# A hybrid encoder layer: branch a's first output block with its token halves interleaved, branch b's operand queued behind the attention, a wider-spaced inverse, another PSUM bank for the last head

## The chip, the cores and the metric

The kernel runs on one core of one Trainium2 chip. The metric is the device time of one execution in microseconds; less is better. TensorE (PE) multiplies matrices, VectorE (DVE), ScalarE (ACT) and GpSimd (POOL) do the elementwise work, and SyncE (SP) issues the DMAs. PEld is the loading of weights into PE, which lies beside the matmuls.

## The reference

One layer over 1024 tokens of width 1024, in float32. One input projection feeds two branches: eight heads of a gated delta rule in chunks of 64 (branch a) and sixteen heads of attention over a band of nine chunks (branch b). Each branch is projected to 1024 columns and merged by gates; then come an output projection, a layer norm, and a feed-forward layer with a short convolution.

```python
h = x * (1.0 + scale_t) + shift_t
proj = h @ w_in
qkv_a, z_a, beta_raw, a_raw, q_b, k_b, v_b, gates = split(proj)
o_a = gated_deltanet(qkv_a, z_a, beta_raw, a_raw, ...)   # per chunk: a triangular solve, then a scan over chunks
o_b = chunk_band_attention(q_b, k_b, v_b, rel_bias)      # softmax over own chunk + previous 8
merged = gate_a * (o_a @ w_branch_a) + gate_b * (o_b @ w_branch_b)
x = layernorm(ALPHA * x + gate_t * (merged @ w_o))
h = x * (1.0 + scale_f) + shift_f
u = causal_dwconv(h @ w_up) + b_conv_ffn                 # width 3
x = layernorm(ALPHA * x + gate_f * ((silu(u_gate) * u_val) @ w_down))
```

## The kernel before

Every large matrix product is made of three: each float32 operand is split into a high part (a cast by ACT into the fast float32 format, `wh`, `hh`, `oah`, `obh`) and a low part (the rest, a subtraction by DVE or POOL, `wl`, `hl`, `oal`, `obl`), and high x high, high x low and low x high are summed in PSUM. `load_split` does this for one block: a DMA of 512 KB into one of three `raw` buffers (`RB`), the cast, the subtraction. `wblock` does it for a block of weights.

The program runs in stages, which overlap:

1. The modulation and the first projections.
2. The eight heads of branch a. While head h goes through its stages, `feed(h + 1)` projects the next head. PE's order is written out by hand: the projections are a stream of units (one matmul of 512 columns is one unit), and at given counts of units a stage is put in as a "wave". A head's waves are `stage_blocks` (copies of 32x32 blocks into `dd`, a transposition into `dt_`), four steps of `stage_inverse` (tiles `pxt`, `py`, `pzz`, `pT`) that build the inverse of a triangular matrix out of its blocks, 22 steps of `stage_chain` (the scan: `pks`, `pvn`, `pu`, `po`), and `stage_out` (the normalised output, transposed by way of `pt`, stored in `oa_d`). `INV0` and `INV00` say where the inverse begins (`INV00` for head 0), `INVS` how far apart its steps are, and the chain is spread evenly from there to the end of the head. The 31 small steps of `stage_solve` on DVE make the blocks' own inverses.
3. The attention of branch b: 64 groups g (head g // 4, two tiles of 128 tokens in each), with scores (`ps`), softmax (DVE's minimum, ACT's exponential), transposes of the weights (`pp`, split into `ph` by ACT and `pl` by DVE) and output (`po`). `fill_to` puts units of other work between these steps, from a list of items: what is left of branch b's own projections, and then the eight blocks of branch a's output projection (`branch_a(j)`, tile `pbr`, 48 units each: 24 for each half of the tokens). A block may start only behind a given group (49 for the first two, 60 for the others). `load(i + 1)` asks for the next item's weights as an item begins. The operand of branch a is read back from `oa_d` in eight parts by `operand(k)`, at the unit counts of `OAT`, counted from the middle of the last projection (`late(15, True)`); 24 is the beginning of `branch_a(0)`. `OL` lists the parts whose low half POOL makes instead of DVE.
4. The rest of `branch_a`, then the eight blocks of branch b's output projection, whose operand `obh`, `obl` is read back from `ob_d` in eight parts after blocks 5, 6 and 7 of `branch_a`.
5. Merge, output projection, layer norm, feed-forward layer, second layer norm.

The order of PE is kept as written from head 0's waves to the end of the attention (`lane.pinned`). On the other engines a scheduler, which simulates the program as it is built, chooses the order. `tc.high_priority` puts a wave's work ahead of others' there. `tc.issue_after(ins)` ties what is issued inside it behind `ins`, on the engine of `ins` alone. A PSUM bank is taken from a ring: `"a"` and `"qkv"` have banks 0 and 1, `"c"` (the chain and `pt`) and `"pt"` (the transposes `pp`) have banks 3 and 4; `turn` holds how often each ring was used.

Lines of the profile that the text speaks of: L190 and L179 subtract the low part (L187 and L176 are their casts; the first pair is for operands and weights loaded in cuts), L184 loads `raw`; L531 issues PE's work in the ordered part, L289 that of branch b's projection; L583 is the last step of the short convolution of q, k and v, L584 its activation; L736 multiplies q by the decay; L770 and L772 copy the blocks, L775 transposes them; L792, L793 and L809 copy results of the inverse; L839 and L845 are steps of the chain; L873 scales its output; L1117 multiplies branch a's block by its gate (tile `ma`), which frees the bank; L1212 and L1216 are the softmax, L1242 and L1243 the split of its transposed weights. The profile names a tile by the buffer that it lies in: G, FT, GT, SA, SB, ST, A, B are shared buffers, and `hh`, `hl` hold branch a's operand from stage 3 on.

Of the kernel before, what the change touches and what calls it, by code (L numbers as in the profile page):

```python
# [12 lines left out]
ALU = mybir.AluOpType  # L13
# [7 lines left out]
NK = 8  # L21
# [14 lines left out]
PTR = 0  # L36
G0 = 3
GA = (3, 2, 2, 2, 2, 2, 1)
INV0, INV00, INVS, OUT0, OUTS, TAIL0 = 38,188,14,14,8,10
WA, WB0 = 9, 10  # L40
EP = (4,12)
OAT = (2, 5, 8, 14, 20, 29, 33, 37)
OL = (1,3,5)
PO = ((1, 5, 2, 3, 7, 6, 4), (1, 5, 2, 3, 7, 6, 4))
ED = ((4,0),(5,0),(5,1),(6,0))
MS = 6
# [93 lines left out]
def hybrid_layer(  # L140
# [547 lines left out]
    def feed(h, n_gates, mods):  # L688

        c = cs[h]  # L690
        decay(h, c)
        k, q = Conv(h, 1), Conv(h, 0)
        c["kT"], c["qT"] = k.y, q.y
        yield from k.half(0)
        yield from k.half(1)
        c["kd"], c["ss"] = big("kd"), sm("ss", 2 * NT)
        yield from q.half(0)
        keys(h, c, 0)
        yield 2
        yield from q.half(1)  # L700
        keys(h, c, 1)
        yield 2
        rates(h, c)
        v = Conv(h, 2)
        c["vT"] = v.y
        mod = mod_rows(mods[0]) if mods else iter(())
        with tc.issue_after(cs[h - 2]["scaled"]) if mods else nullcontext():
            next(mod, None)
        yield from v.half(0)
        c["am"] = big("am")  # L710
        for g in range(2):
            gram(h, c, g)
            yield 4
        blocks_out(h, c)
        if h == 0:
            for key in ("kT", "qT"):
                dump(key, flat(c[key]))
        yield from v.half(1)
        if h == 0:
            dump("vT", flat(c["vT"]))  # L720
        c["at"] = big("at")
        for g in range(2):
            scores(h, c, g)
            yield 4
        c["sz"], szw = big("sz"), wblock(kview(w_in2, 3 * D + h * P, P), NK)
        for n in range(2):
            ps = dhalf(nm("pz"))
            yield from project(ps, szw, n)
            ACT.activation(flat(c["sz"])[:, 512 * n:512 * n + 512], ps, AF.Silu)
            if n == 0:  # L730
                for g in range(2):
                    queries(h, c, g)
                    yield 2
                eq = c["eq"] = sm("eq")
                DVE.tensor_scalar(eq, c["ss"][:, NT:], P * RMS_EPS, P * RMS_EPS * L2_EPS, ALU.mult, ALU.add)
                POOL.tensor_tensor(flat(c["qT"]), flat(c["qT"]), flat(c["gb"]), ALU.mult)  # L736
        c["vs"] = big("vs")
        for g in range(2):
            values(h, c, g)
            yield 2  # L740
        run(mod)
        for i in range(n_gates + 1):
            if i == (h == 1):
                with tc.high_priority(offset=PF):
                    stage_solve(h, c)
            if i < n_gates:
                yield from gate_block(next(gates))
# [13 lines left out]
    def stage_blocks(h, c):  # L761

        fr = c["fr"]
        for b in (1, 3, 0, 2):
            for q in range(4):
                dst = dd[B[b], :, 32 * b + 8 * q:32 * b + 8 * q + 8]
                s_ = fr[B[q], :, 8 * b:8 * b + 8].rearrange("p c t -> p t c")
                with nullcontext() if h else tc.issue_after(cs[1]["ready"]), tc.issue_after(cs[1]["keys"][1]):
                    if q % 2:
                        ACT.copy(dst, s_)  # L770
                    else:
                        DVE.tensor_copy(dst, s_)  # L772
        with tc.issue_after(cs[h - 1]["end"][0] if h else cs[1]["ready"]):
            for b in (1, 3, 0, 2):
                DVE.transpose(dt_[B[b], :, B[b]], dd[B[b], :, B[b]])  # L775
        yield
# [178 lines left out]
    for h in range(HA - 1):  # L955
# [6 lines left out]
        inv, chain = stage_inverse(h, cs[h]), stage_chain(h, cs[h])  # L962
        i0 = INV0 if h else INV00
        waves = [(stage_blocks(h, cs[h]), 0)] + waves if h else [(stage_blocks(h, cs[h]), i0 - 22)]
        waves += [(inv, i0 + INVS * i) for i in range(4)]
        c0 = i0 + 4 * INVS
        gaps = [WB0 if i % 3 == 0 else WA for i in range(22)]
        pos = [sum(gaps[:i]) for i in range(23)]
        waves += [(chain, c0 + (total - TAIL0 - c0) * p / pos[-1]) for p in pos]
# [11 lines left out]
    oah, oal = hh, hl  # L981
    oahk = [oah[:, k, :] for k in range(NK)]
    oalk = [oal[:, k, :] for k in range(NK)]
    vts, ma, keys_low, wb0 = {}, {}, [], []

    class Head:

# [112 lines left out]
    def branch_a(j):  # L1100

        def body(w):
            ma[j] = place(MA[j], [P, S], F32, "ma")
            if j == 0:
                turn["ps_a"] = turn["ps_qkv"]
            if j == 7:
                wb0.append(wblock(kview(wbr[1], 0, P), NK))
            for n in range(2):
                N = slice(512 * n, 512 * n + 512)
                ps = pbank(nm("pbr"), "a")  # L1110
                for u, _ in enumerate(project(ps, w, n)):
                    yield 1
                    if j == 0 and n == 0 and u + 24 in OAT:
                        operand(OAT.index(u + 24))
                gt_ = ma[j][:, N]
                SP.dma_start(gt_, gates_d[j][:, N])
                DVE.scalar_tensor_tensor(gt_, gt_, 1.0, ps, ALU.add, ALU.mult)  # L1117
            for k in {5: (0, 1, 2), 6: (3, 4, 5), 7: (6, 7)}.get(j, ()):
                load_split(obh[k], obl[k], ob_d[k], ACT, DVE)

        return lambda: wblock(kview(wbr[0], j * P, P), NK, cuts=2), body

# [2 lines left out]
    def fills(items):  # L1125

        ws = {}

        def load(i):
            while i < len(items) and i not in ws:  # L1130
                ws[i] = items[i][0]()
                if items[i][2]:
                    return
                i += 1
            while i in ws and not items[i][2]:
                i += 1

        load(0)
        for i, (_, body, units, after) in enumerate(items):
            if units:  # L1140
                load(i + 1)
            while group_no[0] < after:
                yield None
            yield from body(ws.pop(i))
# [124 lines left out]
    def vals(g):  # L1269
# [1 line left out]

    items = [first_pair("q"), first_pair("k"), vals(0), late(1), late(9), late(2), late(10), late(3), vals(1), late(11),
             late(5), vals(2), late(13), late(6), late(14), vals(3), late(7), late(15, True)]
    items += [(*branch_a(j), True, a) for j, a in enumerate((49, 49, 60, 60, 60, 60, 60, 60))]
    fill, done = fills(items), 0

    def fill_to(x):
# [9 lines left out]
    group("MX", "ST", 52)  # L1287
    waves = [(stage_blocks(h, cs[h]), 0)] + [(older, OUT0 + OUTS * i) for i in range(3)]
    inv, chain, last = stage_inverse(h, cs[h]), stage_chain(h, cs[h]), stage_out(h, cs[h])
    waves += [(inv, INV0 + INVS * i) for i in range(4)]  # L1290
    c0 = INV0 + 4 * INVS
    waves += [(chain, c0 + (total - TAIL0 - c0) * p / pos[-1]) for p in pos]
    ready = {}

# [35 lines left out]
    for g in range(8 * NK):  # L1330
# [16 lines left out]
            if h:  # L1347
                seq.insert(0, head(h + 1).load)
        if g == 0:
            seq = [head(1).bias, T[0], lambda: fill_to(done + 4), lambda: wave(last, PC), lambda: fill_to(done + 4),  # L1350
                   lambda: wave(last, PC), lambda: wave(last, PC), lambda: fill_to(done + 4)]
        for key in [k for k in due if g >= min(8 * k[0] + 8 + 2 * k[1], 8 * NK - 1)]:
            finish_part(key)
# [523 lines left out]
```

## Time and profile before

| what | value |
|---|---|
| median of 3 runs | 2171.91 us (2170.02 to 2172.66) |
| the profiled execution | 2167.07 us, span 2165.4 us |
| PE busy | 2108.1 us, 97% of the span |
| DVE, ACT, POOL busy | 1429.3 (66%), 987.7 (46%), 431.9 (20%) us |
| mean granted clock of PE | 0.994 |
| DMA | 263.03 MB, mean 121 GB/s |

The span is the time from the first to the last instruction of the profiled execution. A row of the order of time reads: start, duration, engine, line, operation, result and operands, and in brackets how long the engine had been idle before it and what ended that. A row of the waits reads: who waited, for whom, us in total, how many times, the longest. PE is the engine with next to no idle time, so a wait counts where PE has it; and where its granted clock is below 1, its busy time is longer than it need be.

### The profile page before, as it was taken

Reading aid. Unit: us, or ns where it says so; the run is one execution under the profiler, and the core shown is the slowest. Engines: PE = TensorE matmul, PEld = TensorE weight load, DVE = VectorE, ACT = ScalarE, POOL = GpSimd, SP = SyncE. Lnnn points to the kernel's source line nnn. Section 1 sums busy time; section 2 is a strip of 40 time slices with the busy share of each in tenths; the row PEclk is TensorE's granted clock in tenths of the full one; section 3 lists DMA queues with packets and bytes.
Section 4 is the critical chain, followed back from the end, with each engine's and each line's share of the span. In section 5 each row is a group of like instructions: output and inputs, shape, how many; then the busy total and the mean of one; then the engine's idle time right before and its main releaser. Section 6 shows DMA issues by size and latency. Waiting matters only on the chain. (4 is left out here: it accounts for less than half of the span.)

```text
span 2165.4 us, 31785 instructions
## 1 busy us (share of the span) xinstructions
PE 2108.1 (97%) x11577; PEld 1767.0 (82%) x11577; DVE 1429.3 (66%) x3006; ACT 987.7 (46%) x2159; POOL 431.9 (20%) x385
## 2 busy tenths in 40 slices
PE   7998999999999999999999899999999999999998
PEld 6787788888888888989897778888788888888886
DVE  6478576776777844666556432457997788875754
ACT  5544453454444434566555432235554444452431
POOL 0233233323232321111112124300120000000000
PEclk9999999999999999999999999999999999999999
DMA  9232324323233245554647442422232222275440
GB/s 296 81 89 80 123 76 120 115 74 119 80 104 122 80 125 160 139 136 111 174 120 229 122 142 93 141 88 85 82 98 78 88 88 87 87 282 186 165 156 39
DMA packets 243166, 263.03 MB, mean 121 GB/s; under 512 B 23034, under 2 KB 189491, under 8 KB 243011
## 3 DMA queue, kind: packets, MB, share of 16 engines
q1 hardware_dynamic: 242931, 260.99, 39.0%
q8 instruction: 91, 1.49, 0.3%
q14 instruction: 64, 0.52, 0.1%
q10 hardware_dynamic: 80, 0.03, 0.0%
HBM read 207.89 MB, written 58.83 MB: 123 GB/s over the span
## 5 line engine op out<-in xcount | busy, mean ns | idle before, releaser
L190 POOL TENSOR_TENSOR wl<-raw,wh 128x512 fp32r<-128x512 f32 x170 | 223.8, 1339 | 526.7 <-ACT wh L187 433.3
L1595 PE MATMUL pup<-hh,wop 128*128 128x512 f32 x704 | 224.2, 390 | 0.4 <-ACT G L1632 0.4
L1595 PE MATMUL pup<-t,wop 128*128 128x512 f32 x792 | 189.4, 392 | 1.3 <-DVE cc L1636 0.8
L1595 PEld LDWEIGHTS pup<-t,wop 128*128 128x128 f32 x792 | 148.6, 188 | 34.7 <-DVE cc L1636 1.2
L1749 PE MATMUL pdn<-dop,dop 128*128 128x512 f32 x696 | 161.6, 391 | 0.0
L1595 PEld LDWEIGHTS pup<-hh,wop 128*128 128x128 f32 x704 | 132.2, 188 | 29.0 <-ACT G L1632 0.8
L1749 PEld LDWEIGHTS pdn<-dop,dop 128*128 128x128 f32 x696 | 130.7, 188 | 28.3
L531 PE MATMUL pqkv<-hh,wh 128*128 128x512 f32 x352 | 142.6, 406 | 0.0
L531 PE MATMUL pqkv<-hl,wh 128*128 128x512 f32 x352 | 139.8, 397 | 0.0
L531 PE MATMUL pqkv<-hh,wl 128*128 128x512 f32 x352 | 139.7, 397 | 0.0
L1595 PE MATMUL pup<-hl,wop 128*128 128x512 f32 x352 | 137.2, 390 | 0.0
L187 ACT CAST wh<-raw 128x1024 fp32r<-128x1024 f32 x88 | 92.1, 1047 | 77.9 <-PE pbr L531 18.3
L1637 POOL TENSOR_TENSOR cc<-cc,G 128x512 f32<-128x512 f32 x22 | 44.1, 2004 | 375.6 <-DVE G L1619 352.4
L1216 ACT ACTIVATE G<-G,ST 128x640 f32<-128x640 f32 (+4 forms) x128 | 89.3, 698 | 60.8 <-DVE ST L1212 60.1
L176 ACT CAST wop<-wr 128x512 fp32r<-128x512 f32 x104 | 61.9, 620 | 99.2 <-DVE wr L1577 67.1
L531 PE MATMUL pqk<-hh,wh 128*128 128x512 f32 x256 | 105.9, 414 | 0.0
L531 PE MATMUL pqk<-hl,wh 128*128 128x512 f32 x256 | 104.1, 407 | 0.0
L531 PE MATMUL pqk<-hh,wl 128*128 128x512 f32 x256 | 103.2, 403 | 0.0
L755 DVE TENSOR_TENSOR FT<-FT,G 128x16 f32<-128x16 f32 (+30 forms) x248 | 93.9, 378 | 10.1 <-POOL G L657 2.5
L531 PE MATMUL pgt<-hh,wh 128*128 128x512 f32 x240 | 98.2, 409 | 0.0
L531 PE MATMUL pgt<-hh,wl 128*128 128x512 f32 x240 | 97.5, 406 | 0.0
L1243 DVE TENSOR_TENSOR pl<-pp,ph 128x512 fp32r<-128x512 f32 (+1 forms) x112 | 72.9, 651 | 35.3 <-ACT ph L1242 34.6
(409 smaller groups left out, 5492.6 us busy)
## 6 DMA issues: line engine op xcount, KB each, us to landing
raw<-in_w_in_dram SPq DMA_DIRECT2D x72, 512.0 KB
wr<-in_w_up_dram SPq DMA_DIRECT2D x44, 512.0 KB
dwr<-in_w_down_dram SPq DMA_DIRECT2D x44, 512.0 KB
raw<-in_w_ada_dram SPq DMA_DIRECT2D x32, 512.0 KB
qk_d<-SA SPq DMA_DIRECT2D x80, 128.0 KB
wa<-in_w_ada_dram SPq DMA_DIRECT2D x32, 256.0 KB
gates_d<-GT SPq DMA_DIRECT2D x32, 256.0 KB
g_d<-G SPq DMA_DIRECT2D x15, 512.0 KB
```

The lines of the kernel that those rows point to most:

```text
L176: he.copy(h, src)
L187: he.copy(h, raw)
L190: le.tensor_tensor(l[:, N], raw[:, N], f(h[:, N]), ALU.subtract)
L531: r = getattr(PE, op)(*args, **kw)
L755: DVE.tensor_tensor(pr[:, :, 0:i + 1], ft[:, :, 0:i + 1], fa[:, i:i + 1, 0:i + 1].to_broadcast([P, 8, i + 1]), ALU.mult)
L1216: ACT.activation(sb[:, 0:n], sb[:, 0:n], AF.Exp, bias=mx[:, nb - 1:nb], scale=-1.0, accum_out=total_of(hd, t))
L1243: DVE.tensor_tensor(pl[:, B, :], pp, f(ph[:, B, :]), ALU.subtract).ins)
L1595: i = PE.matmul(ps, a[:, u, k, :], b[v][k], start=(new and k == 0 and u == 0 and v == 0), stop=(k == 3 and u == 1), skip_group_check=not new)
L1637: self.later(7, lambda: POOL.tensor_tensor(o, o, self.t, ADD))
L1749: PE.matmul(ps[n], self.g[:, u, i * P:i * P + P], self.w[v][:, 512 * n:512 * n + 512], start=(first and u == 0 and v == 0), stop=(last and ...
```

## The change

- `branch_a(0)`: both banks are taken at once. The first token half goes through operand parts 0 to 3, then parts 4 to 7 of the first half alternate with parts 0 to 3 of the second (three matmuls each), then parts 4 to 7 of the second. The last three counts of `OAT` are 30, 35 and 40 instead of 29, 33 and 37, and POOL no longer makes the low half of part 1. The weights of `branch_a(1)` are asked for after unit 22 of the block instead of at its beginning.
- Branch b's operand is loaded two parts after each of the blocks 4 to 7 of `branch_a`, with ACT's work tied behind the last traced cast of the attention's transposed weights, and DVE's behind their last subtraction and behind the block's last `ma`.
- The inverse: its four steps begin at 0, 14, 30 and 44 units instead of 0, 14, 28 and 42; for head 0, which begins at 184 instead of 188, at 0, 18, 36 and 50. The chain begins 14 units behind the last.
- Head 1's block copies on DVE are tied behind the last step of head 0's chain.
- The product of L736 is made in two halves of 512 columns.
- In the attention's first group, the last head's `pt` continues with the bank that the ring of `pp` would use next.

```diff
-INV0, INV00, INVS, OUT0, OUTS, TAIL0 = 38,188,14,14,8,10
+INV0, INV00, INVS, OUT0, OUTS, TAIL0 = 38,184,(0,14,30,44),14,8,10
+INVF = (0,18,36,50)
-OAT = (2, 5, 8, 14, 20, 29, 33, 37)
-OL = (1,3,5)
+OAT = (2, 5, 8, 14, 20, 30, 35, 40)
+OL = (3,5)
...
-                POOL.tensor_tensor(flat(c["qT"]), flat(c["qT"]), flat(c["gb"]), ALU.mult)
+                for N in (slice(0, 512), slice(512, 1024)):
+                    POOL.tensor_tensor(flat(c["qT"])[:, N], flat(c["qT"])[:, N], flat(c["gb"])[:, N], ALU.mult)
...
-                with nullcontext() if h else tc.issue_after(cs[1]["ready"]), tc.issue_after(cs[1]["keys"][1]):
+                first_ = cs[1]["ready"] if h == 0 else cs[0]["end"][0] if h == 1 else None
+                with tc.issue_after(first_) if first_ else nullcontext(), tc.issue_after(cs[1]["keys"][1]):
...
-        waves += [(inv, i0 + INVS * i) for i in range(4)]
-        c0 = i0 + 4 * INVS
+        io = INVS if h else INVF
+        waves += [(inv, i0 + i) for i in io]
+        c0 = i0 + io[3] + 14
...
-            for n in range(2):
+            ps = [pbank(nm("pbr"), "a") for n in range(2)] if j == 0 else [None] * 2
+            order = [(n, k) for n in range(2) for k in range(NK)]
+            if j == 0:
+                order = [(0, k) for k in range(4)] + [s_ for k in range(4, NK) for s_ in ((0, k), (1, k - 4))] \
+                    + [(1, k) for k in range(4, NK)]
+            u = 24
+            for n, k in order:
...
+                    if j == 0 and u in OAT:
+                        operand(OAT.index(u))
+                    if j == 0 and u == 46:
+                        next_load[0]()
+                    u += 1
...
-            for k in {5: (0, 1, 2), 6: (3, 4, 5), 7: (6, 7)}.get(j, ()):
-                load_split(obh[k], obl[k], ob_d[k], ACT, DVE)
+            with ExitStack() as st:
+                for i in (*after, last_ma) if j > 3 else ():
+                    st.enter_context(tc.issue_after(i))
+                for k in (2 * j - 8, 2 * j - 7) if j > 3 else ():
+                    load_split(obh[k], obl[k], ob_d[k], ACT, DVE)
...
-            if units:
-                load(i + 1)
+            next_load[0] = lambda i=i: load(i + 1)
+            if units != 2:
+                next_load[0]()
...
-            seq = [head(1).bias, T[0], lambda: fill_to(done + 4), lambda: wave(last, PC), lambda: fill_to(done + 4),
+            seq = [head(1).bias, T[0], lambda: turn.update(ps_c=turn["ps_pt"]),
+                   lambda: fill_to(done + 4), lambda: wave(last, PC), lambda: fill_to(done + 4),
                    lambda: wave(last, PC), lambda: wave(last, PC), lambda: fill_to(done + 4)]
```

More of the change, by code (lines that the diff above doesn't have):

```diff
@@ L983, in hybrid_layer @@
     oalk = [oal[:, k, :] for k in range(NK)]
-    vts, ma, keys_low, wb0 = {}, {}, [], []
+    vts, ma, keys_low, wb0, next_load = {}, {}, [], [], [None]
     class Head:
@@ L1107, in body @@
                 wb0.append(wblock(kview(wbr[1], 0, P), NK))
-            for n in range(2):
-                N = slice(512 * n, 512 * n + 512)
-                ps = pbank(nm("pbr"), "a")
-                for u, _ in enumerate(project(ps, w, n)):
-                    yield 1
[L1113 to L1117, printed above, removed]
-            for k in {5: (0, 1, 2), 6: (3, 4, 5), 7: (6, 7)}.get(j, ()):
-                load_split(obh[k], obl[k], ob_d[k], ACT, DVE)
+            ps = [pbank(nm("pbr"), "a") for n in range(2)] if j == 0 else [None] * 2
[5 more added lines that the diff above has]
+            for n, k in order:
+                N = slice(512 * n, 512 * n + 512)
+                if ps[n] is None:
+                    ps[n] = pbank(nm("pbr"), "a")
+                for a, r in ((w[0], hhk), (w[0], hlk), (w[1], hhk)):
+                    lane.matmul(ps[n], a[:, k, :], r[k][:, N], start=(k == 0 and a is w[0] and r is hhk),
+                                stop=(k == NK - 1 and a is w[1]))
+                    yield 1
+                    if j == 0 and u in OAT:
[3 more added lines that the diff above has]
+                    u += 1
+                if k == NK - 1:
+                    gt_ = ma[j][:, N]
+                    SP.dma_start(gt_, gates_d[j][:, N])
+                    last_ma = DVE.scalar_tensor_tensor(gt_, gt_, 1.0, ps[n], ALU.add, ALU.mult).ins
+            with ExitStack() as st:
[3 more added lines that the diff above has]
+                    load_split(obh[k], obl[k], ob_d[k], ACT, DVE)
         return lambda: wblock(kview(wbr[0], j * P, P), NK, cuts=2), body
@@ L1273, in hybrid_layer @@
              late(5), vals(2), late(13), late(6), late(14), vals(3), late(7), late(15, True)]
-    items += [(*branch_a(j), True, a) for j, a in enumerate((49, 49, 60, 60, 60, 60, 60, 60))]
+    items += [(*branch_a(j), 1 + (j == 0), a) for j, a in enumerate((49, 49, 60, 60, 60, 60, 60, 60))]
     fill, done = fills(items), 0
@@ L1289, in hybrid_layer @@
     inv, chain, last = stage_inverse(h, cs[h]), stage_chain(h, cs[h]), stage_out(h, cs[h])
-    waves += [(inv, INV0 + INVS * i) for i in range(4)]
-    c0 = INV0 + 4 * INVS
+    waves += [(inv, INV0 + i) for i in INVS]
+    c0 = INV0 + INVS[3] + 14
     waves += [(chain, c0 + (total - TAIL0 - c0) * p / pos[-1]) for p in pos]
```

## The prediction

> **What bounds the kernel now.** I read the page first (busy shares), then a table of stretches with the granted clock, then what TensorE (PE) waited for, and last the order of time around each wait.
>
> ```profile
> span 2165.4 us, 31785 instructions
> PE 2108.1 (97%) x11577; PEld 1767.0 (82%) x11577; DVE 1429.3 (66%) x3006; ACT 987.7 (46%) x2159; POOL 431.9 (20%) x385
> ```
>
> PE bounds the kernel: 97% busy, 57 us idle. The change removes no matmul, so it can only win back idle time, and busy time in which PE ran below full speed. The stretches show where that is (columns: length; busy us and count of PE, PEld, DVE, ACT, POOL; granted clock; DMA share; GB/s):
>
> ```profile
> 186.20:190.40 4.20, 4.17 (x57) 3.37 (x58) 3.68 (x18) 3.69 (x19) 0.00 (x0) 0.59 0.02 4
> 1173.70:1180.40 6.70, 5.64 (x15) 4.05 (x16) 3.77 (x9) 2.81 (x5) 1.73 (x2) 0.51 0.95 278
> 1181.00:1211.00 30.00, 30.00 (x186) 26.30 (x184) 16.93 (x50) 17.16 (x39) 7.24 (x6) 1.00 0.61 169
> 1221.70:1228.00 6.30, 5.70 (x23) 5.05 (x24) 3.08 (x9) 2.41 (x7) 0.00 (x0) 0.50 0.43 138
> 1228.00:1262.00 34.00, 34.00 (x183) 28.82 (x182) 13.38 (x35) 10.69 (x24) 3.83 (x3) 1.00 0.14 48
> 1279.50:1282.70 3.20, 3.11 (x7) 2.51 (x8) 0.63 (x2) 0.40 (x1) 0.45 (x1) 0.51 0.87 284
> ```
>
> Four places run at about half clock, each right behind a wait. What such a place costs beyond its wait is busy time times the missing share of clock: 4.17 x 0.41 = 1.7, 5.64 x 0.49 = 2.8, 5.70 x 0.50 = 2.85, 3.11 x 0.49 = 1.5 us. The waits (total, times, longest), first of 150 to 800 us, then of 1150 to 1310, and one between:
>
> ```profile
> PE pzz L531 <- ACT am L809: 5.2, 6, 1.4
> PE py L531 <- ACT G L793: 2.9, 1, 2.9
> PE pvn L531 <- DVE vs L839: 2.2, 1, 2.2
> PE pq L531 <- DVE at L668: 0.6, 1, 0.6
> PE pt L531 <- DVE pl L1243: 1.8, 1, 1.8
> PE pp L531 <- DVE pl L1243: 6.1, 3, 4.1
> PE pbr L531 <- DVE ma L1117: 3.6, 1, 3.6
> PE po L531 <- DVE B L1243: 1.5, 1, 1.5
> PE pp L531 <- ACT G L1216: 1.4, 2, 1.1
> PE pbr L531 <- ACT hh L187: 0.9, 2, 0.5
> PE pbr L531 <- POOL hl L190: 0.9, 1, 0.9
> PE pbr L531 <- DVE hl L190: 0.2, 1, 0.2
> ```
>
> Every part of the change touches one of these rows. A matmul of 512 columns is one unit of the hand-written order and costs
>
> ```profile
> 1308.50 87.47 PE pbr L289 x384
> ```
>
> 87.47 / 384 = 0.228 us.
>
> **The change part by part.**
>
> *Head 0's inverse and the split POOL product.* Why py waits 2.9 us:
>
> ```profile
> 176.15 1.84 DVE L775 STREAM_TRANSPOSE G<-G 32x256 f32<-32x256 f32 x4
> 178.34 0.70 PE L531 MATMUL pxt<-G,am 128*32 128x32 f32 x32
> 181.70 2.63 DVE L583 TENSOR_TENSOR tmp<-tmp,SM 128x3 f32<-128x3 f32 x1
> 181.95 2.36 POOL L736 TENSOR_TENSOR y<-y,tmp 128x1024 f32<-128x1024 f32 x1
> 184.42 0.63 ACT L584 ACTIVATE tmp<-tmp 128x512 f32<-128x512 f32 x1 [6.19 <-DVE FT L755]
> 185.80 0.37 ACT L793 ACTIVATE G<-pxt 32x256 f32<-32x256 f32 x1
> ```
>
> A three-element DVE addition takes 2.63 us and ends with the POOL product (184.33 and 184.31). ACT's L584 needs it, and L793, which py needs, stands behind L584 on ACT. Halving the product lets DVE in after some 1.2 us, so I move L793 from 186.2 to about 185.0. pxt goes 4 units (0.9 us) forward, py stays at unit 202, so py, asked for at 183.3 now (2.9 before L793's end), is asked for at about 183.6 when pxt's own new wait is counted: a wait of 1.4 instead of 2.9. That gains 1.5, and the 1.7 of half clock, since the 2.2 us wait for vs in this trace lost none. Against it, pxt is now asked for at 177.4 and DVE's transposes end at 178.0: 0.9 of new wait, of which the pq wait gives back 0.6. Sum +2.9 us. Bounds: -0.3 (ACT's order as it is, both halves ahead of the addition) to +4.3 (L793 ahead of L584). Two POOL halves for one cost a second start per head; POOL is 20% busy, and no engine waited on L736: nothing. Without that cover it would cost at most the product again, 2.4 us.
>
> *Head 1's block copies behind head 0's chain.*
>
> ```profile
> 208.23 3.66 DVE L772 COPY G<-FT 32x64 f32<-32x64 f32 x7
> 209.48 2.48 ACT L770 COPY G<-FT 32x64 f32<-32x64 f32 x8
> ```
>
> Seven copies stand ahead of vs (L839) on DVE; behind `cs[0]["end"][0]` they don't. The wait is tied on DVE only, so ACT's eight still stand ahead of the next vn copy and give back about 0.8 of 2.2: +1.4, bounds 0 to 2.2. Late next are the copies themselves, some 3.7 us of DVE work for head 1's pxt, which stands behind the whole output stage of head 0: covered; without that cover they cost their 3.7.
>
> *More room before pzz.* Six heads wait 5.2 in all; two units each give 6 x 0.456 = +2.7. The chain starts two units later and ends where it did, 1% less room per step: nothing, cover being the fills between its steps. Bounds -0.5 (the chain's small waits grow by that) to 2.7.
>
> *The last head's bank.*
>
> ```profile
> 836.33 3.74 DVE L873 TENSOR_SCALAR at<-at,SM 128x128 f32<-128x128 f32 x8 [1.75 <-POOL SM L521]
> 840.33 0.54 DVE L1243 TENSOR_TENSOR pl<-pp,ph 128x384 fp32r<-128x384 f32 x1
> ```
>
> The first transposes wait for pl's bank until 840.9; in the other bank they need only four of the eight scalings, done at 838.2, and PE is there 1.8 earlier, at 839.1. The second four, four units (0.9 us) and a set of transposes behind, come to the first bank at 840.4, about 0.5 us early: 1.8 - 0.5 = +1.3, bounds 0 to 1.8.
>
> *Branch a's first block.* Operand blocks k = 4 to 7 are needed at units 12, 18, 24, 30 instead of 12, 15, 18, 21, and the next block's weights are asked for after unit 22 instead of ahead of k = 5.
>
> ```profile
> 1157.78 2.89 DVE L190 TENSOR_TENSOR hl<-raw,hh 128x512 fp32r<-128x512 f32 x2 [0.16 <-ACT hh L187]
> 1165.86 1.05 ACT L187 CAST wh<-raw 128x1024 fp32r<-128x1024 f32 x1 [0.75 <-DMA raw<-in_w_branch_a_dram]
> 1171.80 1.03 ACT L187 CAST hh<-raw 128x1024 fp32r<-128x1024 f32 x1
> 1176.18 1.05 ACT L187 CAST hh<-raw 128x1024 fp32r<-128x1024 f32 x1 [0.26 <-DMA raw<-oa_d]
> ```
>
> The cast at 1165.86 is that of the next block's weights; its 512 KB, its cast and its POOL half stand ahead of k = 5 (cast 1171.80) and k = 7 (1176.18) in the three raw buffers, on SP's queue, ACT and POOL. Moved behind them, k = 5 comes one buffer turn, some 4 us, earlier, while its need moves 3 units and more later: the operand waits 0.9 + 0.9 + 0.2 and most of the softmax wait of 1.1, a DVE subtraction in front of the scores, should go. Of 3.0 us idle and 2.8 of clock I keep 1.0 for what the softmax still asks: +4.8, bounds 0 to 5.8. The weights, asked for about 1171 and needed at unit 48 near 1185, have some 14 us for a transfer of 4.3 (below), a cast of 1.05 and POOL's half, bounded by the 2.89 above: nothing, and what is late beyond 14 if that fails. The second half's bank is needed at unit 15: rivals. `OL` gives DVE the low half of k = 1 in POOL's place: two more subtractions on DVE, but the two in the first row took 2.89 beside POOL. I book +0.5 of the 1.5 us wait for po; bounds -1.3 to 1.5.
>
> *Branch b's operand, in the attention's end.*
>
> ```profile
> 1214.40 0.37 SPq L184 DMA_DIRECT2D raw<-ob_d  x1
> 1218.73 1.04 ACT L176 CAST ob<-raw 128x1024 fp32r<-128x1024 f32 x1 [3.63 <-DMA raw<-ob_d]
> ```
>
> The cast of a block of branch b's operand stands at the head of ACT for 3.63 us, for a transfer issued 4.3 before, and the softmax's casts stand behind it: the 4.1 and 0.5 of the pp row, then 2.85 of half clock. Behind the last turn's cast it can't. The head's first groups have no fill, so 1.2 of softmax latency stays: +6.2, bounds 0 to 7.4.
>
> *The same operand, in branch a's last blocks.*
>
> ```profile
> 1275.39 3.43 DVE L179 TENSOR_TENSOR ob<-raw,ob 128x1024 fp32r<-128x1024 f32 x2 [6.83 <-ACT ob L176]
> 1278.85 1.29 DVE L1117 SCALAR_TENSOR_TENSOR ma<-ma,pbr 128x512 f32<-128x512 f32 x2
> 1287.38 1.22 DVE L179 TENSOR_TENSOR ob<-raw,ob 128x1024 fp32r<-128x1024 f32 x1
> ```
>
> Two subtractions, waiting for their casts, hold `ma`, which frees PE's bank. Queued behind each block's last `ma`, two a block, they cannot hold that block's own: +3.6 + 1.5 = 5.1, bounds 0 to 5.1. Late next are blocks 6 and 7, behind branch a's last `ma`: two subtractions of 1.22 and that `ma`, 0.65, end 3.1 us after PE starts on branch b, and k = 6 is first read 19 units, 4.3 us, after it: nothing, with 1.2 to spare.
>
> Sum: 2.9 + 1.4 + 2.7 + 1.3 + 4.8 + 0.5 + 6.2 + 5.1 = 24.9; with all upper bounds 30.8. The profiled execution took 2167.07 (2165.4 of span), so 2142.2 of its own time. The median of the runs shown stands 4.8 above that execution, and I take the sum off the median, 2171.9 - 24.9 = 2147.0.
>
> *A rule weighed.* The half clock at 187 follows a wait of 2.9 us. By the Trainium skill, "TensorE: Matmul & The Clock Gate", "Part 1: The HAM clock gate", the clock is halved after an idle window of about 3.4 us; by that a 2.9 us wait would not cost it, and the sum would be 1.7 less, 23.2. The trace disagrees (clock 0.59 there), and I keep the row.
>
> **The rivals.**
>
> *The operand is late instead.* Two raw buffers hold a pair until the subtractions behind `ma`, and only then is the next pair loaded. For a pair that is 2.4 of subtracting, 4.3 of transfer and 2.1 of casts, 8.8, against 10.9 of a block (48 units): it fits by 2.1. With the subtractions at 3.43 a pair and transfers of 6, it doesn't, and branch b starts into a wait of about 5 plus 1.5 of clock: 2153.5. For it: the DMA share of 0.87 in the stretch from 1279.5, while such loads ran; against it: the first pair can be loaded in the attention already, and the next pairs have a block each.
>
> *The first block still waits.* It now needs its second bank at unit 15, near 1171, and the last projection's output leaves that bank by DVE work behind the operand's subtractions. A wait there eats that block's 5.3: 2152.3. Against it: those subtractions come earlier now.
>
> *The change does little of what it says*: the engines' order is a scheduler's, and casts are put ahead of the softmax or of `ma` elsewhere. Then branch b's 6.2 + 5.1 are lost: 2158.3; if branch a's 5.3 too, 2163.6. If every wait returns at the next bank, it is within 0.2% (4.3 us, about what a measurement of this kernel can tell from no change).
>
> *Slower, by the clock.* The last head's first groups have no fill. If their remaining waits let the clock fall and keep it there, 34.00 busy us of 1228 to 1262 run at half: +34, 2147 + 34 = 2181. It decides from 25 + 4.3 = 29 us of full-speed work at half. For it: 5.70 busy us at 0.50 behind these waits. Against it: after 1228 the clock was 1.00 with PE 34.00 of 34.00 busy. The Trainium skill's same page, "A second HAM failure mode: psum-queue depth-cycling", has a clock that oscillates where matmuls go round the banks with small idles between; the new first block changes its bank every three matmuls. In 1181 to 1211 of this trace, scores, transposes and projections alternate banks at 1.00.
>
> **How the numbers follow.** The forecast 0.57 (its own range 2141 to 2152), operand late 0.11, first block waits 0.10, little done 0.06: faster 0.84. Returned waits, no change: 0.09. Clock: 0.07. The range starts at 2171.9 - 30.8 = 2141 and reaches the last of the faster cases, 2164; outside lie 0.16 and a little of the forecast.
>
> **What would show it.** Right: no half-clock stretch near 187, 1175, 1222 and 1275; the pzz, py and vs rows gone or under 3 us together; no ob cast on ACT before the attention's last ph; `ma` never behind ob on DVE. Wrong: a pbr wait at L289 for ob (operand late), a pbr wait for the projection's SA output (bank), a pxt wait over 1 us, or a clock under 1.00 for more than 10 us after 1211.

## The result, and the profile after

The changed kernel takes 2149.81 us (median of 4 runs, 2147.80 to 2150.53), the kernel before, run beside it, 2172.28: a ratio of 0.9896, interval 0.9879 to 0.9913. That is 22.5 us less; 24.9 were forecast, and 2147.0 as the time.

The two profiled executions stand closer: a span of 2147.7 against 2165.4 us, 17.7 apart. The one after (2149.37 us) is like its median, the one before (2167.07) was shorter than its own median. Keep the two differences apart; half of what follows lies between them. Every time and ratio here is of undisturbed runs: of the experiments' runs, one of 2323 us at a granted clock of 0.85 and one of the kernel before of 9135 us are left out.

The page of the changed kernel, its first two lines:

```profile
span 2147.7 us, 31798 instructions
PE 2101.4 (98%) x11577; PEld 1762.4 (82%) x11577; DVE 1428.9 (67%) x3008; ACT 988.3 (46%) x2159; POOL 430.8 (20%) x391
```

PE does the same 11577 matmuls in 6.7 us less, and its idle time went from 57 to 46 us: both kinds of gain that the prediction looked for. The longest of PE's waits, in 150 to 800 us and then in 1150 to 1310:

```profile
PE py L532 <- ACT G L796: 2.6, 1, 2.6
PE pzz L532 <- ACT am L812: 2.0, 4, 0.9
PE pks L532 <- DVE SA L857: 1.8, 1, 1.8
PE pu L532 <- ACT SA L848: 1.2, 5, 0.2
...
PE pp L532 <- DVE pl L1264: 6.3, 3, 3.7
PE po L532 <- DVE B L1264: 0.9, 1, 0.9
```

The waits for `vs`, `ma`, `hh` and `hl` are gone, pzz is down from 5.2 to 2.0. But `py` still waits 2.6, `pks` waits 1.8 where it waited 0.5, `pu` is new, and one wait of `pp` is 3.7. The stretches (columns as before: granted clock, DMA share and GB/s close the row):

```profile
186.50:190.50 4.00, 3.94 (x62) 3.28 (x63) 3.52 (x17) 3.87 (x21) 0.00 (x0) 1.00 0.02 4
1165.20:1169.00 3.80, 3.46 (x14) 3.13 (x15) 2.61 (x8) 2.91 (x6) 1.01 (x1) 0.58 0.82 230
1205.00:1216.00 11.00, 8.00 (x62) 7.16 (x61) 7.88 (x24) 8.15 (x21) 3.76 (x3) 1.00 0.59 200
1262.00:1292.00 30.00, 30.00 (x134) 24.82 (x133) 14.05 (x14) 9.47 (x9) 10.46 (x6) 1.00 0.49 158
```

Of the four half-clock places one is left, in branch a's first block. In the attention's end 3 us of idle time remain, at full clock, and in branch a's last blocks PE is busy 30.00 of 30.00 us.

The start of one and the same matmul, compared in both traces, gives each place its share of the 17.7:

| place | forecast | profile against profile |
|---|---|---|
| head 0: its inverse, the halves, the tie | 2.9 + 1.4 | 2.2 |
| heads 1 to 6: room before pzz | 2.7 | 1.3 |
| last head: the other bank | 1.3 | 0.6 |
| `OL`, the wait of po at 1157 | 0.5 | 0.6 |
| branch a's first block | 4.8 | 1.9 |
| attention's end and branch a's last blocks | 6.2 + 5.1 | 6.2 + 5.3 |
| the start, where nothing was edited, and the rest | 0 | -0.4 |

### The profile page after: what moved, and what is told of

The parts are those of the page before. It is cut to its first block, busy times and chain, and to the rows that moved or that the text cites. A ratio compares the mean times of both kernels' runs of the same rounds, so it can differ in the third digit from the quotient of the medians.

```text
span 2147.7 us, 31798 instructions
## 1 busy us (share of the span) xinstructions
PE 2101.4 (98%) x11577; PEld 1762.4 (82%) x11577; DVE 1428.9 (67%) x3008; ACT 988.3 (46%) x2159; POOL 430.8 (20%) x391
## 4 chain that ended last, share of the span: by engine, by line
PE 84%; DVE 8%; ACT 3%; DMA 2%; issue 2%; SPq 1%; POOL 0%; DVEq 0%; ACTq 0%; POOLq 0%
PE pup L1617 17%; PE pdn L1771 11%; PE pqkv L532 7%; PE pqk L532 6%; PE pgt L532 6%; PE pv L532 5%; PE pwo L1459 4%; PE pbr L290 4%; PE pbr L532 4%; PE po L532 4%; PE pz L532 4%; PE ps L532 3%; PE pp L532 2%; PE pfirst L290 1%; DMA raw<-in_w_in_dram 1%
## 5 line engine op out<-in xcount | busy, mean ns | idle before, releaser
L757 DVE TENSOR_TENSOR FT<-FT,G 128x16 f32<-128x16 f32 (+30 forms) x248 | 92.1, 371 | 8.9 <-POOL G L658 2.5
```

The costliest lines, as they stand in the source:

```text
L757: DVE.tensor_tensor(pr[:, :, 0:i + 1], ft[:, :, 0:i + 1], fa[:, i:i + 1, 0:i + 1].to_broadcast([P, 8, i + 1]), ALU.mult)
```

## The experiments

Each kernel was timed beside the kernel before, whose median there lay between 2169.89 and 2174.48 us. So where two experiments are compared, the ratio to the kernel before counts more than the microseconds; the changed kernel's is 0.9896 (0.9879 to 0.9913).

**Branch b's operand alone**, on the kernel before.

```diff
-            for k in {5: (0, 1, 2), 6: (3, 4, 5), 7: (6, 7)}.get(j, ()):
-                load_split(obh[k], obl[k], ob_d[k], ACT, DVE)
+            with ExitStack() as st:
+                for i in (*after, last_ma) if j > 3 else ():
+                    st.enter_context(tc.issue_after(i))
+                for k in (2 * j - 8, 2 * j - 7) if j > 3 else ():
+                    load_split(obh[k], obl[k], ob_d[k], ACT, DVE)
```

> The kernel before with one edit: branch b's operand loaded two parts after each of blocks 4 to 7, tied behind the attention's last split and the block's last ma. Theory (each place pays by itself): the waits of 4.1 + 0.5 at 1222 and 3.6 at 1279 and their half clock (2.85 and 1.5) go, 1.2 of softmax wait stays: 11.3 us less than before, no ob cast on ACT before the attention's end. Rival (the whole pays only together, since a late part of one place is caught up in the next): 5 us less or under.

2157.52 us (2155.30 to 2158.85), ratio 0.9925 (0.9912 to 0.9937): 15.2 us by the medians, two thirds of the whole change from one edit. The longest waits of 1150 to 1310 in its trace:

```profile
PE pp L531 <- DVE pl L1246: 2.7, 2, 1.5
PE po L531 <- DVE B L1246: 1.5, 1, 1.5
PE pp L531 <- ACT G L1219: 1.4, 2, 1.1
```

`ma` is gone, and of the 4.1 and 0.5 of `pp` nothing is left: the mechanism is as forecast. That it is worth 15.2 and not 11.3 is in part explained by kernels in which this code is as before. The same cast waited as follows in the order of time of the first-block kernel, the room kernel and the tie kernel (all three below):

```profile
1221.37 1.04 ACT L176 CAST ob<-raw 128x1024 fp32r<-128x1024 f32 x1 [6.51 <-DMA raw<-ob_d]
```

```profile
1223.60 1.04 ACT L177 CAST ob<-raw 128x1024 fp32r<-128x1024 f32 x1 [4.70 <-DMA raw<-ob_d]
```

```profile
1223.46 1.04 ACT L176 CAST ob<-raw 128x1024 fp32r<-128x1024 f32 x1 [6.34 <-DMA raw<-ob_d]
```

6.51, 4.70 and 6.34 us, against 3.63 in the profiled execution of before. PE's wait followed it: 6.97, 5.15 and 6.79 against 4.08. So the execution that the prediction read had a short wait there, by 1.1 to 2.9 us. That does not carry the whole excess of 3.9. From 1205 to 1300 us, matmul against matmul, these three kernels take 1.6 us more, 0.7 less and 3.0 more than that execution; and the trace of this edit's own kernel gains 9.9 us there, 4.6 in the attention's end (where a half clock behind a wait of 1.47, near 1216, cost it 1.2) and 5.3 in branch a's last blocks. Where the rest of the 15.2 lies, no trace here shows.

**Branch a's first block alone** (interleaving, `OAT`, `OL`, the later request for the weights), on the kernel before.

```diff
-OAT = (2, 5, 8, 14, 20, 29, 33, 37)
-OL = (1,3,5)
+OAT = (2, 5, 8, 14, 20, 30, 35, 40)
+OL = (3,5)
...
+                order = [(0, k) for k in range(4)] + [s_ for k in range(4, NK) for s_ in ((0, k), (1, k - 4))] \
+                    + [(1, k) for k in range(4, NK)]
```

> The kernel before with one edit: branch a's first block interleaved, with its counts, its POOL parts and its later load of the next weights. Theory, from the trace of the changed kernel: the operand's waits go, but the casts of parts 3 and 4 stand on ACT waiting for their DMA (3.4 and 1.4 us there) ahead of the softmax, so PE gets a wait of some 3.7 us and half clock behind it: 1 to 2 us less than before. Rival (the prediction's term, and the new wait comes from another edit): 5.3 us less.

2167.97 us (2163.10 to 2170.12), ratio 0.9972 (0.9961 to 0.9984): 4.8 us by the medians. Its longest row of waits from 1150 to 1310:

```profile
PE pp L531 <- DVE pl L1257: 12.4, 4, 7.0
```

No `hh` or `hl` is waited for, so the operand is in time. But the 12.4 of `pp` hold a new wait of 3.43 in this block (the 7.0 is the unedited one of branch b's operand). The changed kernel has the same, and its order of time says why:

```profile
1154.26 0.58 SPq L185 DMA_DIRECT2D raw<-oa_d  x1
1156.88 0.53 SPq L185 DMA_DIRECT2D raw<-oa_d  x1
1159.29 1.05 ACT L188 CAST hh<-raw 128x1024 fp32r<-128x1024 f32 x1 [3.37 <-DMA raw<-oa_d]
1162.52 1.04 ACT L188 CAST hh<-raw 128x1024 fp32r<-128x1024 f32 x1 [1.39 <-DMA raw<-oa_d]
1164.09 0.59 ACT L1263 CAST ph<-pp 128x512 fp32r<-128x512 f32 x1
1165.54 0.90 PE L532 MATMUL pp<-ident,G 128*128 128x128 f32 x3 [3.69 <-DVE pl L1264]
```

Two casts of operand parts, asked for 5.0 and 5.6 us before, wait on ACT for their transfers, and the softmax's cast `ph` stands behind them on the same queue. PE takes the next transposes when `ph` and `pl` are done. It is the fault that the change cures in the attention's end, made anew 50 us earlier.

**The operand's parts 3 to 7 brought later**, on the changed kernel.

```diff
-OAT = (2, 5, 8, 14, 20, 30, 35, 40)
+OAT = (2, 5, 8, 18, 25, 31, 36, 41)
```

> The changed kernel with the units at which operand parts 3 to 7 are brought moved from (14, 20, 30, 35, 40) to (18, 25, 31, 36, 41), so that the softmax cast stands ahead of the two operand casts on ScalarE's queue that waited 3.37 and 1.39 us for their transfers. Theory (in-order ScalarE waits for a DMA with latency-critical work behind it): the 3.69 us wait of pp at 1165 shrinks below 1 us and the clock stays at 1.00 there; 3 to 5 us faster than the changed kernel, 2145 to 2147. Rival (the operand is then late for branch a's first block): waits of pbr for hh or hl of 2 to 4 us come back, 2149 to 2153.

2150.24 us (2148.79 to 2151.55), ratio 0.9897 (0.9885 to 0.9910): no gain. Both theories missed: the wait did not shrink as a whole, and no `pbr` wait came.

```profile
1157.93 1.05 ACT L188 CAST hh<-raw 128x1024 fp32r<-128x1024 f32 x1 [4.07 <-DMA raw<-oa_d]
1161.66 0.55 PE L532 MATMUL pp<-ident,G 128*128 128x128 f32 x3 [1.86 <-DVE pl L1264]
1174.92 1.04 ACT L188 CAST wh<-raw 128x1024 fp32r<-128x1024 f32 x1 [4.04 <-DMA raw<-in_w_branch_a_dram]
1177.32 0.66 PE L532 MATMUL pp<-ident,G 128*128 128x128 f32 x4 [2.71 <-ACT G L1237]
```

and a stretch of the same trace:

```profile
1165.00:1178.00 13.00, 10.29 (x57) 8.55 (x57) 6.84 (x18) 7.38 (x14) 3.53 (x4) 0.96 1.07 281
```

3.69 became 1.86, and 2.71 came up at 1177, where the cast of the next block's weights waits 4.04 us for its transfer with the softmax behind it. 1.86 + 2.71 is 4.57. The stretch has the DMA queues full (share 1.07, 281 GB/s). Which cast waits can be chosen; that some cast on ACT's queue waits for these 512 KB blocks was not removed by it. That the transfers are the limit here is read from that share and not shown by a run with fewer bytes.

**The inverse's room alone**, on the kernel before.

```diff
-INV0, INV00, INVS, OUT0, OUTS, TAIL0 = 38,188,14,14,8,10
+INV0, INV00, INVS, OUT0, OUTS, TAIL0 = 38,184,(0,14,30,44),14,8,10
+INVF = (0,18,36,50)
```

> The kernel before with one edit: the inverse's steps at 0, 14, 30, 44 (head 0 from 184 at 0, 18, 36, 50). Theory, from the trace of the changed kernel: the waits of pzz fall from 5.2 to about 2, the chain gives about 1.5 of it back in waits for ACT, py still waits 2.5 and more: 1 to 2 us less, up to 3.5 if the half clock at 187 goes. Rival (nothing is given back): 4.5 us less.

2174.25 us (2171.10 to 2181.28, 11 runs), ratio 1.0013 (1.0002 to 1.0024): nothing won. Its waits from 150 to 800 us:

```profile
PE pu L532 <- ACT SA L846: 3.1, 10, 0.4
...
PE py L532 <- ACT G L794: 2.4, 1, 2.4
PE pks L532 <- DVE SA L855: 1.8, 1, 1.8
PE pzz L532 <- ACT am L810: 1.7, 3, 0.9
```

pzz falls from 5.2 to 1.7 as forecast, and `pu` (3.1) and `pks` (1.3 more) take it all.

**The room undone**, on the changed kernel (the same lines, the other way).

> The changed kernel with the waves of the inverse back at their old units (start 188, step 14 in all heads). Theory (the room moves the waits rather than removing them): pzz waits 4.5 to 5.5 us again, pu and pvn waits go down by about as much, 2148 to 2151. Rival (the prediction's term of 2.7 us holds inside the whole change): 2152 to 2153.

2153.41 us (2151.73 to 2157.55), ratio 0.9917 (0.9904 to 0.9929): slower than the changed kernel by 3.6 us by the medians and 4.6 by the ratio, though the ratios' intervals still overlap. Its longest waits from 150 to 800 us:

```profile
PE pzz L531 <- ACT am L811: 7.0, 6, 1.5
PE py L531 <- ACT G L795: 3.0, 1, 3.0
PE pu L531 <- ACT SA L847: 2.0, 6, 0.8
```

The rival holds: inside the whole change the room is worth something, alone it is not. So another edit makes the difference, and the next runs name it.

**The tie, the halves and the bank**, on the kernel before.

> The kernel before with three edits: head 1's copies tied behind head 0's chain, the POOL product in two halves, the last head's bank. Theory: the bank gives 1.4, the tie about 1 to 2, the halves nothing, since they run back to back and the small DVE addition still ends with the second: 2.5 to 3.5 us less, the addition (L583) still over 2.4 us. Rival (the halves let DVE in between): the addition near 1.4 us, py's wait under 1.8, 5.5 us less.

2169.77 us (2167.76 to 2174.70, 11 runs), ratio 0.9992 (0.9983 to 1.0000): 3.0 by the medians, 1.7 by the ratio. In its trace the wait for `vs` is gone (0.76 of `pu` in its place), and the last head's wait for its bank is 0.41 where it was 1.77. `py` still waits 3.0.

**The product whole again**, on the changed kernel, and **the same issued behind the values step**.

```diff
-                for N in (slice(0, 512), slice(512, 1024)):
-                    POOL.tensor_tensor(flat(c["qT"])[:, N], flat(c["qT"])[:, N], flat(c["gb"])[:, N], ALU.mult)
+                POOL.tensor_tensor(flat(c["qT"]), flat(c["qT"]), flat(c["gb"]), ALU.mult)
```

> The changed kernel with GpSimd's head-0 product as one 1024-column instruction again; against the changed kernel's 2149.8. Theory (the halves run back to back and the small vector addition ends with the second one, so halving buys nothing): py still waits 2.4 to 3.1 us at 182, time 2149 to 2151; the five waits of pu of 0.24 us either stay (then they belong to the spread of the inverse) or go (then they belong to the halves, which doubled the product in every head; time about 2148.5). Rival (halving is what took the half clock away after that wait): py wait 2.9, clock about 0.6 behind it, 2151.5 to 2152.7.

> The changed kernel with GpSimd's head-0 product whole and issued behind the values step, so that it does not run beside the three-element vector addition. Theory (that addition took 2.79 us because it ran beside GpSimd's product): the addition takes under 0.3 us, py's wait at 182 falls from 2.56 to under 0.5 us, 2147 to 2148. Rival (the addition waits for something else, or G is late for the next step by the later product): a wait of 2 to 3 us stays at py or moves to pxt, 2149 to 2152.

2154.53 us (2152.07 to 2159.45), ratio 0.9922 (0.9908 to 0.9936), and 2154.55 (2154.16 to 2155.60), ratio 0.9918 (0.9905 to 0.9931). Moving the product in the program did not move it in time: POOL started it beside the addition as ever, so the second kernel is a repeat of the first. The first theory had the wait of `py` right and the time wrong, the second neither: `py` waits as long as before (2.44, 2.42), and yet both kernels are 4.7 us slower by the medians, 5.6 and 4.8 by the ratio. The two longest waits of the first, from 150 to 800 us:

```profile
PE pu L532 <- ACT SA L847: 3.1, 10, 0.4
PE py L532 <- ACT G L795: 2.4, 1, 2.4
```

`pu` waits ten times instead of five, the five new ones 0.37 to 0.41 us each. DVE and ACT near one of them, first with the product whole, then in the changed kernel:

```profile
292.57 2.39 POOL L737 TENSOR_TENSOR y<-y,tmp 128x1024 f32<-128x1024 f32 x1 [5.53 <-PE pq L532]
295.28 0.16 DVE L736 TENSOR_SCALAR SM<-SM 128x8 f32<-128x8 f32 x1
295.40 0.27 DVE L756 TENSOR_TENSOR FT<-FT,G 128x104 f32<-128x104 f32 x1
295.71 0.26 DVE L758 TENSOR_REDUCE FT<-FT 128x8 f32<-128x104 f32 x1
295.89 1.22 DVE L601 TENSOR_TENSOR tmp<-tmp,SB 128x1024 f32<-128x1024 f32 x1
```

```profile
290.70 2.54 POOL L738 TENSOR_TENSOR y<-y,tmp 128x512 f32<-128x512 f32 x2 [5.31 <-PE pq L532]
293.56 0.16 DVE L736 TENSOR_SCALAR SM<-SM 128x8 f32<-128x8 f32 x1
293.68 0.27 DVE L757 TENSOR_TENSOR FT<-FT,G 128x104 f32<-128x104 f32 x1
293.87 1.22 DVE L601 TENSOR_TENSOR tmp<-tmp,SB 128x1024 f32<-128x1024 f32 x1
```

In the changed kernel L601 stands between the multiplication (L757) and the reduction of a step of the block inverses; with the whole product it stands behind both (L756, L758). It starts 0.61 us behind L736 there and 0.31 here, and counted from PE's own progress (the `pvn` of 221 is 1.42 us later in that execution) it is 0.60 later. Behind L601 ACT has a chain without a gap, two activations, a table load and a cast, and then the copy of `pvn` that `pu` needs. Without the inverse's room the whole product brings no such wait: the kernel before has none of `pu`.

The halves also do, beside other products, what the prediction hoped for at `py`. Steps of the block inverses beside head 0's product, in the changed kernel and then with the product whole:

```profile
129.79 1.17 DVE L757 TENSOR_TENSOR FT<-FT,G 128x48 f32<-128x48 f32 x1
131.24 0.98 DVE L757 TENSOR_TENSOR FT<-FT,G 128x56 f32<-128x56 f32 x1
```

```profile
131.97 2.05 DVE L756 TENSOR_TENSOR FT<-FT,G 128x64 f32<-128x64 f32 x1
```

Such a step takes 0.23 us or less with nothing beside it. With halves, one ends just behind the first half (1.29 us from 129.61), and the next with the second; the whole product holds one step to its own end. Beside the products of heads 2 to 7 the changed kernel's rows read alike (0.81 to 1.12 us a step). So the waits of `pu` go with the halves, by way of when L601 comes on VectorE; how much of that is this gap and how much the order that the scheduler chose, no run separates.

**The halves in head 0 alone**, on the changed kernel.

```diff
-                for N in (slice(0, 512), slice(512, 1024)):
+                for N in (slice(0, 512), slice(512, 1024)) if h == 0 else (slice(0, 1024),):
```

> The changed kernel with the product in halves in head 0 alone, and whole in heads 1 to 7; against the changed kernel's 2149.8. Theory (halving pays in heads 1 to 7, by the order that it gives VectorE there: six waits of pu of 0.36 to 0.41 us for ScalarE's copy of pvn, each some 0.6 us of a head): those six waits are there again, 2153 to 2154.5. Rival (it pays in head 0, as the prediction had it): no such waits, 2149 to 2151.

2152.61 us (2151.71 to 2153.10), ratio 0.9902 (0.9886 to 0.9917): 2.8 slower by the medians, but 1.3 by the ratio, within the noise; and `pu` waits ten times again, five of them 0.37 to 0.41 us. The theory's count was six; its place is right, since the waits go by the halves of heads 1 to 7.

**Head 0's and head 1's product on DVE**, on the changed kernel, one at a time.

```diff
-                    POOL.tensor_tensor(flat(c["qT"])[:, N], flat(c["qT"])[:, N], flat(c["gb"])[:, N], ALU.mult)
+                    (DVE if h == 1 else POOL).tensor_tensor(flat(c["qT"])[:, N], flat(c["qT"])[:, N], flat(c["gb"])[:, N], ALU.mult)
```

> The changed kernel with head 0's product (both halves) on VectorE in place of GpSimd, so that nothing runs on GpSimd beside the three-element addition. Theory (the addition's 2.79 us is GpSimd's product): the addition takes 0.15 to 0.3 us and py's wait falls from 2.56 to 0.3 to 1.5 us (two VectorE halves of about 0.7 us may stand ahead); what is gained there is partly taken by the wait of pks for SA behind it (1.78 us), so 2148 to 2150. Rival (the addition waits for its inputs, not for GpSimd): py waits 2.4 us or more as before and the halves come on top, 2151 to 2153.

> The changed kernel with head 1's product (both halves) on VectorE in place of GpSimd. The product that stands at 182 us beside the three-element addition is head 1's, not head 0's; on VectorE's queue its halves stand behind that addition. Theory (the addition's 2.79 us is GpSimd's product beside it): the addition takes 0.15 to 0.3 us and py's wait falls from 2.56 to under 0.6 us; part of it comes back in the wait of pks for SA behind it (1.78 us), where VectorE now has two halves of 0.68 us more: 2147 to 2149.5. Rival (the addition waits for its inputs): it still takes 2.5 us or more, py waits 2.5 us, 2149.5 to 2152.

The first (DVE with `h == 0`; 2148.11 us in three runs, 2146.13 to 2151.53, ratio 0.9877, 0.9856 to 0.9898) missed its aim: head 0's product runs at 130 us, and the one beside the addition is head 1's. The addition still took 2.82 us there, and `py` waited 1.6. The second gave 2147.78 us (2146.64 to 2148.84), ratio 0.9890 (0.9873 to 0.9907). The addition in the changed kernel, and then in this one, with a stretch of the granted clock:

```profile
182.34 2.79 DVE L584 TENSOR_TENSOR tmp<-tmp,SM 128x3 f32<-128x3 f32 x1
182.61 2.50 POOL L738 TENSOR_TENSOR y<-y,tmp 128x512 f32<-128x512 f32 x2
```

```profile
181.22 0.32 DVE L584 TENSOR_TENSOR tmp<-tmp,SM 128x3 f32<-128x3 f32 x1
201.34 0.49 PE L532 MATMUL pks<-SA,y 128*128 128x128 f32 x2 [2.14 <-DVE SA L857]
```

```profile
201.30:205.50 4.20, 4.16 (x13) 3.45 (x14) 3.71 (x10) 0.27 (x1) 0.00 (x0) 0.59 0.06 20
```

Without the product beside it the addition takes 0.32 us, and `py` waits no more. That is shown. But of the 2.56 us only 0.3 reach the next stage: counted from pq at 180, the `pvn` at 220 is 0.3 us earlier. `pks` now waits 2.14, `pu` 0.29, and the half clock behind `pks` costs 4.16 x 0.41 = 1.7. By the ratio the kernel can't be told from the changed one. No version was found that clearly beats it.

**The tie undone**, on the changed kernel.

```diff
-                first_ = cs[1]["ready"] if h == 0 else cs[0]["end"][0] if h == 1 else None
+                with nullcontext() if h else tc.issue_after(cs[1]["ready"]), tc.issue_after(cs[1]["keys"][1]):
```

> The changed kernel without the tie of head 1's copies behind head 0's end. Prediction's term: 1.4 us (bounds 0 to 2.2), with pvn waiting 2.2 us for vs again, 2151 to 2152. Theory now (pks waits 1.78 us in the changed kernel where it waited 0.46 before, so the tie moves most of the wait): pvn waits 2.2, pks under 0.6, 2149.5 to 2150.8.

2151.68 us (2148.82 to 2154.76), ratio 0.9898 (0.9882 to 0.9914): 1.9 slower by the medians, 0.4 by the ratio, so the two can't be told apart by time. In the trace `pvn` waits 2.75 for `vs` again, and `pks` 0.89 instead of 1.78.

All the traces together show how the room and the halves work on each other. From 250 us to 828, which is heads 1 to 6 and a part of the last, each kernel's time between the same two matmuls is compared with that in the profiled execution of before. The two kernels with neither edit (branch b's operand, the first block) take 0.3 and 0.5 us less. The four with the room and the whole product in these heads (the room alone, the product whole and its repeat, the halves in head 0 alone) take 1.5 to 6.6 more. The two with the halves and no room (the tie kernel, the room undone) take 2.3 and 4.1 more. The five with both take 1.7 less to the same. So either edit alone loses there, and only the two together do not.

## Why the prediction was right or wrong

The sign, the bound (PE, through its waits and the clock behind them) and the main mechanism, branch b's operand, were right; the forecast of 2147.0 missed by 2.8. That is a better hit than its steps were. Four of them failed. Two of the errors nearly cancel, and that much of the hit is luck: on the trace that was read the gains were summed too high, and between the medians the change won more than on that trace.

- *"Halving the product lets DVE in after some 1.2 us"*, booked at `py`. At this addition it doesn't: the two halves run back to back, 2.50 us in all, and the addition, begun 0.27 us ahead of them, still ends with the second. `py` waits 2.56, not 1.4. That the clock stayed at 1.00 behind it won no time either: with the whole product it was halved there (3.47 busy us at 0.51 behind 188), and at `pks`, 18 us later, that kernel stands where the changed one does, because `pks` waits 0.33 in it and 1.78 here. The wait behind took up the loss. The prediction added a gain at `py` without asking which wait ends last in head 0's stretch. It also booked "no engine waited on L736: nothing". In the trace that it read, steps of the block inverses on DVE took 2.21 us beside head 0's product and 2.34 beside head 7's, for some 0.2 otherwise. Undoing the halves in heads 1 to 7 or in all brings back five waits of `pu` and costs 2.8 to 4.7 us by the medians, 1.3 to 5.6 by the ratio.
- *"More room before pzz ... +2.7."* Alone it gave nothing, since `pu` and `pks` took it. The lower bound of -0.5 named the cause, "the chain's small waits grow", and mis-sized it. The room was paid only together with the halves, 1.3 us in heads 1 to 6 of the profiled pair; either alone lost there, in every trace. Each edit was costed alone, and these two are not additive: +1.5 for the one and -3.0 for the other with its two neighbours, but 3.6 and 4.7 lost when either is taken out of the whole.
- *"+4.8, bounds 0 to 5.8"*, the first block. The operand's waits went, as forecast. "... most of the softmax wait of 1.1 ... should go": it did not, it grew to 3.69 us, because the prediction looked for late DVE work and not for the casts on ACT that wait for a DMA, though it had named just that in the attention's end. Profile against profile the block gave 1.9 (with `OL` 2.6 of 5.3); by the medians of the edit alone 4.8. The second is nearer the forecast, with a wide interval (3.5 to 8.5 us), and the first is likely low: from 1152 to 1188 us, the kernels in which this block is unedited take 0.2 (branch b's operand), 1.8 (the room) and 2.3 us (the tie) more than the execution that was read. The size stays open between the two; that the block still waits, and for what, does not.
- *"The median stands 4.8 above that execution, and I take the sum off the median."* A sum over one execution's waits can be taken off another only if the waits are the same there. They were not: the wait for branch b's operand was 1.1 to 2.9 us longer in three other executions, and between 1152 and 1300 us two of these, where nothing is edited there, take 1.1 and 5.3 us more than the one that was read. The edit alone measured 15.2 for a term of 11.3; profile against profile the same places gave 11.5 in the changed kernel and 9.9 in this edit's own. So the sum was too high by 6.8 on its own trace (24.9 against 18.1 without the start), and by 2.4 between the medians, because the median of before holds some 5 us that the execution read did not. Where all of these lie, no trace shows.

Right by their own steps: 6.2 + 5.1 for branch b's operand (6.2 + 5.3 on the profiled pair), with PE never waiting for `ma`; the bank (1.77 to 0.41, of which 0.8 went to new waits for `am` in the same head); `OL` (0.6). The two subtractions that wait for `ma` now run beside full PE work:

```profile
1262.74 0.69 DVE L1134 SCALAR_TENSOR_TENSOR ma<-ma,pbr 128x512 f32<-128x512 f32 x1 [7.20 <-PE pbr L532]
1263.34 3.45 DVE L180 TENSOR_TENSOR ob<-raw,ob 128x1024 fp32r<-128x1024 f32 x2
1266.72 0.68 DVE L1134 SCALAR_TENSOR_TENSOR ma<-ma,pbr 128x512 f32<-128x512 f32 x1
```

Of the rivals none came as described: no wait for `ob` in branch b, none at the second bank (the first block did wait, but for the softmax), and no clock below 1.00 behind 1211 while PE had work. Of the signs that should show it right, three failed: the half clock near 1167; `pzz` and `py` with 4.6 us together instead of under 3; and the last row above, a `ma` right behind two subtractions of `ob`, which cost PE nothing.

What stays open: what sets the pace of head 0's chain, where `pks` takes whatever `py` gives up; why two halves let DVE in beside other products and not at this addition; and whether fewer or earlier bytes would end the wait in the first block.

## What to carry to other kernels

On an engine that takes its queue in order, as ACT did in the rows above, a cast that waits for a DMA holds everything behind it; queue it behind the latency-critical work, and read such a wait from several executions, since it varies. A wait that goes is worth only what the next one does not take: follow the work to the next stage's first matmul before booking it. Edits that share a stage are costed together, and an edit that only splits an instruction may pay where nobody looked, so compare the rows beside every instance of it, and the order that the scheduler chose.

## What the hardware did that was not expected

A GpSimd product held VectorE's two-input operations up, and in two instructions it let them in at one place and not at another. A three-element addition issued 0.27 us ahead took 2.79 us beside the two halves, 2.65 beside one whole product, and 0.32 without. A step of the block inverses, issued 0.18 us behind the start of the first half, took 1.17 and ended with that half; beside a whole product such a step took 2.05.

The clock does not go by the length of a wait alone. It was halved behind waits of 2.44 us (product whole), 2.14 (head 1's product on DVE) and 1.47 (branch b's operand alone, near 1216), and stayed at 1.00 behind 2.56 in the changed kernel, at the same `py`, behind the same 1.47 in its row of 1205 to 1216, and behind 3.24 in the first block of the kernel with the room undone. Nor does it go by the code: the changed kernel waited 1.78 for `pks` and kept full clock, and the one with the operand brought later, which is the same up to there, waited 1.82 and then had 5.20 busy us at 0.67. An execution of the changed kernel can so lose some 1.7 us (5.20 x 0.33) at head 0 that the profiled one kept. The rule of the Trainium skill that the prediction weighed ("TensorE: Matmul & The Clock Gate", "Part 1: The HAM clock gate", an idle window of about 3.4 us) agrees with none of these waits that halved it. It agrees with those that did not, and with the 3.69 in the changed kernel's first block, which did. By it the prediction's sum would also have lost what it kept of the 2.8 of clock near 1175, where no wait was longer than 1.1, and not the 1.7 alone.

The wait for one and the same 512 KB load lay between 3.63 and 6.51 us in four executions of kernels that are alike there.
